# Seven-product gate and up blocks in three more feed-forward halves, and adaLN steps placed by an account of VectorE time

## The chip, the cores and the metric

One core of one Trainium2 chip runs the whole program. The metric is device time in microseconds (us) of one execution; medians are over repeated runs. TensorE (PE) does the matmuls, VectorE (DVE) and ScalarE (ACT) the elementwise work, GpSimd (POOL) a few small steps, and SyncE (SP) issues nearly all DMAs.

## The reference

Two layers over x of 512 tokens by 1024 channels, in float32. Each layer is a feed-forward half-step, a mixer (a convolution module in layer 0, pooling and block attention in layer 1), and a second feed-forward half-step. Every one of these sub-layers is normalised, shifted and scaled by vectors that come from a conditioning vector c (adaLN):

```
cond = silu(c)
for i in range(2):
    mod = (cond @ ada_w[i] + ada_b[i]).reshape(1, 3, 3, 1024)       # shift, scale, gate of 3 sub-layers
    h = rms_norm(x, ffn_norm[i, 0]) * (1 + mod[:, 0, 1]) + mod[:, 0, 0]
    x = x + 0.5 * mod[:, 0, 2] * ((silu(h @ w_gate) * (h @ w_up)) @ w_down)    # 1024 -> 2816 -> 1024
    ... mixer with mod[:, 1], then the second feed-forward half with mod[:, 2]
out = rms_norm(x, final_norm)
```

The four feed-forward halves are called parts 1 to 4 here: parts 1 and 2 belong to layer 0, parts 3 and 4 to layer 1. `ada_w` is 1024 x 9216 for each layer: nine chunks of 1024 columns, two of which (shift and scale of the first half) are computed at the start of the program.

## The kernel before, in words

Activations are kept transposed, as eight tiles of 128 channels by 512 tokens. Every operand of a matmul is split in a high and a low part (`hh`/`hl`, `th`/`tl`, `whi`/`wlo`), and each product is three matmuls: high by high, high by low, low by high (`mac`, L269). ScalarE makes the high part of a weight tile (L258), VectorE the low part (L260).

A feed-forward half is done in three sections of 8, 6 and 8 strips of 128 of the 2816 columns (`SECTIONS`). In a section each gate and each up strip is an item of 24 matmuls over 512 tokens (8 tiles x 3), then eight down items follow, 24 matmuls each (18 in the section of six strips). The post of an up item multiplies by silu of gate and splits the result into `th` and `tl` (L650 to L652); the post of a down item adds to x (L928), and in the last section also starts a sum of squares (L512). The last two down items belong to the boundary, which computes the next norm.

`run` (L131) writes out the order by hand: it walks a plan of steps, and every engine executes its own instructions in the order in which they were emitted. Before an item's matmuls it runs deferred work (`tick`), and issues the splits of up to three items ahead (`AHEAD`), with four weight tiles (`W_BUFS`). Loads of 1 MB go to four raw buffers (`RAW_BUFS`) on SP's queue, in the order in which they are first used; load i waits until load i-4 has been used.

An adaLN chunk is seven steps (`ada_steps`, L438): four that each multiply two rows of weights by c and add them up on VectorE (L454, L456), a fold (transpose L467, reduce L469), an empty one, and one that sums over partitions with a matmul (L474), which is followed by small adds (`put_mod`, L482). These steps are put between items as background: `body` (L935) hands out one after each item until the list is empty.

Part 4 already computes gate and up of 16 of its 22 strips as seven-product blocks (`pair_run`, L764): gate and up by the two halves of the 1024 channels, times those halves by two halves of the tokens, is a 2 x 2 by 2 x 2 product, made with seven products instead of eight. A product is 4 tiles x 3 matmuls over 256 tokens (`seventh`, L747), so a block is 84 matmuls of 256 columns where gate and up together are 48 of 512. VectorE makes the sums of weights and splits them (L727 to L744), subtracts and adds the products (L798, L805), and multiplies (L817). The sums of activations are made once per half, by `forms` (L691), and the first block of a run is prepared by `lead_in` (L829) beside the items ahead of it.

Of the kernel before, what the change touches and what calls it, by code (L numbers as in the profile page):

```python
# [14 lines left out]
P = 128  # L15
# [13 lines left out]
AHEAD = 3  # L29
# [38 lines left out]
class Trunk:  # L68
# [62 lines left out]
    def run(self):  # L131
# [6 lines left out]
        for dry in (True, False):  # L138
# [27 lines left out]
            ring = []  # L166
            for st in self.plan:
# [145 lines left out]
    def setup(self):  # L313
# [8 lines left out]
        cp = self.cp  # L322

# [23 lines left out]
        crow = cp.tile([8, P], F32, name="crow")  # L347
# [6 lines left out]
        par = cp.tile([P, P], F32, name="par")  # L354
        taps = cp.tile([A_CONV * 4, P], F32, name="taps")
        adab = cp.tile([72, 2, P], F32, name="adab")
# [81 lines left out]
    def ada_steps(self, l, s, ch):  # L438
# [97 lines left out]
    def apply(self, i, k, sl, rb):  # L536
# [3 lines left out]
        if n == S:  # L540
            t = self.fp.tile([P, n], F32, name=f"t{n}", tag="t512", bufs=3)
# [134 lines left out]
    def pair_items(self, l, s, first):  # L676
# [14 lines left out]
    def forms(self, kk):  # L691
# [8 lines left out]
        t = [self.fp.tile([P, 2, 256], F32, name="yy", tag="yy", bufs=2) for _ in range(2)]  # L700
# [4 lines left out]
        for e in range(2):  # L705
            hi = self.fp.tile([P, 2, 256], F32R, name=f"fh{kk}{e}", tag=f"fh{kk}{e}", bufs=1)
            lo = self.fp.tile([P, 2, 256], F32R, name=f"fl{kk}{e}", tag=f"fl{kk}{e}", bufs=1)
# [56 lines left out]
    def pair_run(self, pairs, prev, nxt, down, bg=()):  # L764

        nc = self.nc
        low = lambda p, n: (lambda: p.lows[n]())
        half = lambda p, n, c: (lambda: self.split_half(p, n, self.flat(p)[:, c * S:(c + 1) * S]))

        def begin(p):  # L770
            self.plan.append(("call", lambda: self.sums13(p), [p.raw]))

        def put_a(p):
            self.plan.append(("slot", p.a, lambda: self.split_full(p, ("a11", "a12"), self.flat(p)[:, 0:1024])))

        def put_c(p):
            self.plan.append(("slot", p.c, lambda: self.split_full(
                p, ("s3", "s1"), p.s13.rearrange("p a b -> p (a b)"))))
# [18 lines left out]
        def u2(p):  # L797
            nc.vector.tensor_tensor(p.x[:, 256:512], p.x[:, 256:512], p.p1, op=ALU.subtract)  # L798
            p.y = self.fp.tile([P, 2, 256], F32, name="yy", tag="yy", bufs=2)
# [25 lines left out]
        def do(*fns):  # L825
            for fn, *args in fns:
                self.call(lambda fn=fn, args=args: fn(*args))

        def lead_in(p):  # L829

            return [lambda: (begin(p), put_a(p), do((low(p, ("a11", "a12")),))),
                    lambda: (do((self.sum2, p), (half(p, "s2", 0),), (self.sum4, p)),),
# [864 lines left out]
```

## Time and profile before

| | us |
|---|---|
| median of 3 runs (1911.03 to 1911.79) | 1911.08 |
| the profiled execution | 1910.01 |
| its span, first to last instruction | 1908.2 |
| TensorE busy | 1856.6 |
| VectorE busy | 1183.8 |
| ScalarE busy | 681.3 |

The span is what the trace shows; the execution's own time is 1.8 us more. Busy times are unions of an engine's instructions. Matmuls are pipelined, so their durations overlap, and distances between their starts say more than durations. In a timeline the first number is the start, the second the duration; in brackets stands the idle time of the engine before it and what ended it.

### The profile page before, as it was taken

The page shows a single profiled execution, that of the slowest core. Times are in us where ns is not written, and L with a number is a line of the kernel's source. Part 1 is how long each engine was busy: PE and PEld are TensorE (multiplying, and loading weights), DVE is VectorE, ACT ScalarE, POOL GpSimd, SP SyncE. Part 2 cuts the span into 40 slices and gives each one's busy share as a digit, 9 for nine tenths or more (in the row PEclk, how much of TensorE's full clock was granted, in tenths as well). Part 3 has the DMA queues.
Part 4 walks back from the last instruction along what each step waited for, and adds up shares of the span by engine and source line. Part 5 has one row for each costly group of instructions (what it writes and reads, how often), then busy time and mean ns, then how long its engine had stood idle before and what let it go on. Part 6 is the DMA issues. An engine that isn't in the chain of part 4 may idle for free.

```text
span 1908.2 us, 22872 instructions
## 1 busy us (share of the span) xinstructions
PE 1856.6 (97%) x9290; PEld 1534.0 (80%) x9290; DVE 1183.8 (62%) x1652; ACT 681.3 (36%) x1084; POOL 131.8 (7%) x107
## 2 busy tenths in 40 slices
PE   5999999999979999999999999999999999999998
PEld 4788888888768888888888888888876688898997
DVE  6666676468976666663366643333757577576874
ACT  4321222235544322222242222223554444253553
POOL 2100000005550000000000000000102000000000
PEclk7999999999989999999999999999999999999999
DMA  9556656423221566562326542323122122424231
GB/s 252 171 203 214 205 195 215 158 67 111 67 88 45 199 216 200 201 199 89 111 67 221 200 142 78 110 89 107 54 84 71 45 89 67 133 62 138 79 100 45
DMA packets 221617, 247.29 MB, mean 130 GB/s; under 512 B 4572, under 2 KB 202056, under 8 KB 221512
## 3 DMA queue, kind: packets, MB, share of 16 engines
q1 hardware_dynamic: 221380, 245.78, 40.3%
q8 instruction: 73, 1.20, 0.3%
q14 instruction: 32, 0.26, 0.0%
q10 hardware_dynamic: 132, 0.05, 0.0%
HBM read 243.72 MB, written 2.10 MB: 129 GB/s over the span
## 4 chain that ended last, share of the span: by engine, by line
PE 88%; DVE 7%; ACT 2%; DMA 1%; issue 1%; POOL 1%; SPq 0%; ACTq 0%; DVEq 0%; POOLq 0%
PE bank L273 26%; PE bank L275 25%; PE bank L274 25%; PE bank L758 7%; DVE hl L549 1%; DVE bank L1051 1%; PE bank L1318 1%; DMA raw<-in_ada_w_dram 1%; DVE wlo L260 1%; DVE t L544 1%; PE bank L1271 1%; PE bank L1297 1%; ACT whi L258 1%; DVE yb L983 0%; PE bank L1184 0%
## 5 line engine op out<-in xcount | busy, mean ns | idle before, releaser
L273 PE MATMUL bank<-hh,whi 128*128 128x512 f32 (+1 forms) x1504 | 575.8, 383 | 5.6 <-ACT hh L547 3.2
L274 PE MATMUL bank<-hl,whi 128*128 128x512 f32 (+1 forms) x1504 | 569.5, 379 | 8.1 <-DVE hl L549 8.1
L275 PE MATMUL bank<-hh,wlo 128*128 128x512 f32 (+1 forms) x1504 | 568.4, 378 | 2.5 <-DVE wlo L260 2.5
L260 DVE TENSOR_TENSOR wlo<-raw,whi 128x1024 fp32r<-128x1024 f32 (+1 forms) x275 | 334.6, 1223 | 154.6 <-ACT whi L258 153.0
L258 ACT CAST whi<-raw 128x1024 fp32r<-128x1024 f32 (+1 forms) x285 | 289.0, 1020 | 208.6 <-PE bank L274 182.4
L273 PE MATMUL bank<-th,whi 128*128 128x512 f32 (+1 forms) x896 | 336.1, 375 | 5.1 <-ACT whi L258 4.5
L275 PE MATMUL bank<-th,wlo 128*128 128x512 f32 (+1 forms) x896 | 333.1, 372 | 5.4 <-POOL wlo L260 5.4
L273 PEld LDWEIGHTS bank<-hh,whi 128*128 128x128 f32 x1504 | 284.1, 189 | 66.8 <-ACT hh L547 3.3
L274 PEld LDWEIGHTS bank<-hl,whi 128*128 128x128 f32 x1504 | 283.8, 189 | 66.6 <-DVE hl L549 9.6
L274 PE MATMUL bank<-tl,whi 128*128 128x512 f32 (+1 forms) x896 | 332.9, 372 | 0.2 <-DVE tl L1324 0.2
L275 PEld LDWEIGHTS bank<-hh,wlo 128*128 128x128 f32 x1504 | 283.7, 189 | 61.2 <-DVE wlo L260 3.7
L273 PEld LDWEIGHTS bank<-th,whi 128*128 128x128 f32 x896 | 169.0, 189 | 38.9 <-ACT whi L258 5.6
L275 PEld LDWEIGHTS bank<-th,wlo 128*128 128x128 f32 x896 | 169.0, 189 | 38.5 <-POOL wlo L260 6.6
L928 DVE SCALAR_TENSOR_TENSOR x<-bank,modG,x 128x512 f32<-128x512 f32 (+1 forms) x124 | 86.2, 699 | 183.2 <-PE bank L275 182.6
L274 PEld LDWEIGHTS bank<-tl,whi 128*128 128x128 f32 x896 | 169.4, 189 | 31.9 <-DVE tl L1324 0.5
L650 DVE TENSOR_TENSOR m<-bank,sg 128x512 f32<-128x512 f32 (+1 forms) x75 | 50.2, 670 | 185.7 <-PE bank L275 178.0
L651 ACT CAST th<-m 128x512 fp32r<-128x512 f32 (+1 forms) x75 | 45.3, 604 | 307.0 <-DVE m L650 307.0
L456 DVE SCALAR_TENSOR_TENSOR adaacc<-raw,cond,adaacc 128x1024 f32<-128x1024 f32 x112 | 143.5, 1282 | 2.3
L644 ACT ACTIVATE sg<-bank 128x512 f32<-128x512 f32 (+1 forms) x78 | 44.0, 564 | 222.1 <-PE bank L275 222.1
L526 POOL TENSOR_TENSOR rs<-ms,mhalf 128x2 f32<-128x2 f32 x12 | 8.4, 699 | 1551.2 <-DVE ms L525 1551.2
L508 ACT ACTIVATE sq<-x 128x512 f32<-128x512 f32 (+1 forms) x54 | 29.0, 537 | 127.1 <-DVE x L928 125.4
L547 ACT ACTIVATE hh<-t,modB 128x256 fp32r<-128x256 f32 (+1 forms) x88 | 45.5, 528 | 63.1 <-DVE t L544 63.1
(249 smaller groups left out, 1985.6 us busy)
## 6 DMA issues: line engine op xcount, KB each, us to landing
raw<-in_ada_w_dram SPq DMA_DIRECT2D x64, 1024.0 KB, 5.0
raw<-in_ffn_w_gate_dram SPq DMA_DIRECT2D x35, 1024.0 KB, 5.4
raw<-in_ffn_w_up_dram SPq DMA_DIRECT2D x35, 1024.0 KB, 6.4
raw<-in_ffn_w_down_dram SPq DMA_DIRECT2D x32, 1024.0 KB, 5.3
raw<-in_ffn_w_down_dram SPq DMA_DIRECT2D x16, 768.0 KB, 4.4
raw<-in_conv_w_in_dram SPq DMA_DIRECT2D x10, 1024.0 KB, 5.1
raw<-in_ffn_w_gate_dram SPq DMA_DIRECT2D x18, 512.0 KB, 4.3
raw<-in_ffn_w_up_dram SPq DMA_DIRECT2D x18, 512.0 KB, 5.3
```

Source lines behind the costliest of these rows:

```text
L258: self.nc.scalar.copy(hi[:, 0:n, :], w)
L260: low = lambda eng=eng, lo=lo, hi=hi, w=w, n=n: eng.tensor_tensor(lo[:, 0:n, :], w, hi[:, 0:n, :].bitcast(F32), op=ALU.subtract)
L273: nc.tensor.matmul(ps, lhsT=it.hi[k], rhs=xh[:, sl], start=start, stop=False)
L274: nc.tensor.matmul(ps, lhsT=it.hi[k], rhs=xl[:, sl], start=False, stop=False)
L275: nc.tensor.matmul(ps, lhsT=it.lo[k], rhs=xh[:, sl], start=False, stop=stop)
L456: nc.vector.scalar_tensor_tensor(acc, r.tile[:, j, :], self.cond[:, k:k + 1], acc, op0=ALU.mult, op1=ALU.add)
L547: nc.scalar.activation(self.hh[k][:, sl], t, AF.Identity, bias=b, scale=1.0)
L644: nc.scalar.activation(self.sg[slot][:, sl], ps[:, sl], AF.Silu)
L650: nc.vector.tensor_tensor(m[:, sl], ps[:, sl], self.sg[slot][:, sl], op=ALU.mult)
L651: nc.scalar.copy(self.th[slot][:, sl], m[:, sl])
L758: mm = lambda w, x, start=False: nc.tensor.matmul(ps, lhsT=w, rhs=x, start=start, stop=False, skip_group_check=True)
L928: nc.vector.scalar_tensor_tensor(self.x[d][:, sl], ps[:, sl], self.modG[:, i, d:d + 1], self.x[d][:, sl], op0=ALU.mult, op1=ALU.add)
```

## The change

Parts 1, 2 and 3 now call `swiglu_pairs` too, with 12, 16 and 14 blocks: the last n strips of each section, given as counts such as (2, 6, 8). Part 4 keeps its 16. The function `swiglu` is gone.

adaLN steps carry a cost in us of VectorE. `slack` is called behind each ordinary item with the time that is taken to be free there (3.7 for a gate or up item, 3.6 or 2.2 for a down item, less the cost of a `forms` or `lead_in` step put there, and 3.0 once behind a run of blocks), and hands out steps as long as the account covers their cost, at most two with a load at a time, none behind a fold. Steps go through a queue (`drain`), which issues them when their load has been issued; it is stopped during a run of blocks (`hold`). What is left at the end of a part is called one after another. Part 1 computes six chunks instead of seven, the convolution stage one instead of none, part 2 four instead of six, part 3 five instead of three. The fold is done in two halves of 512 columns with its reductions at once, and several tiles share tags or are smaller (`SPARE`, `yy`, `qhi`), so that the tiles of blocks and adaLN fit side by side.

```diff
+FOLD = 1.9
+SPARE = [f"f{i}" for i in range(16)]
...
+            ring, queue, held = [], [], False
+
+            def drain(every=False):
+
+                while queue and not held and (every or queue[0][2] is None or queue[0][2].tile is not None):
+                    _, fn, r, cost = queue.pop(0)
+                    if r is not None:
+                        uses[id(r)] -= 1
+                    fn()
+                    if cost == FOLD:
+                        if every:
+                            self.tick()
+                        else:
+                            break
+                    pump()
...
+                        drain()
...
+                elif st[0] == "beside":
+                    if dry:
+                        if st[2] is not None:
+                            touch(st[2])
+                    else:
+                        queue.append(st)
+                        drain()
+                elif st[0] == "hold":
+                    held = st[1]
+                elif st[0] == "sync":
+                    if not dry:
+                        drain(True)
...
-            steps.append((accumulate(r, kk), r))
+            steps.append((accumulate(r, kk), r, 2.3))
 
         def fold():
 
-            tr = self.fp.tile([P, D], F32, name="adatr", tag="adatr", bufs=2)
-            nc.vector.transpose(tr, st["acc"])
             st["r"] = r = self.fp.tile([P, 32], F32, name="adar", tag="adar")
-            self.defer(lambda: nc.vector.tensor_reduce(
-                r, tr.rearrange("p (b j) -> p b j", j=32), axis=AX.X, op=ALU.add))
+            for e in range(2):
+                tr = self.fp.tile([P, S], F32, name="yy", tag="yy", bufs=2)
+                nc.vector.transpose(tr, st["acc"][:, e * S:(e + 1) * S])
+                nc.vector.tensor_reduce(r[:, 16 * e:16 * e + 16], tr.rearrange("p (b j) -> p b j", j=32),
+                                        axis=AX.X, op=ALU.add)
 
         def reduce():
             ps = self.bank()
             nc.tensor.matmul(ps[:, 0:32], lhsT=self.sel, rhs=st["r"], start=True, stop=True)
             self.defer(lambda: self.put_mod(l, s, ch, ps))
 
-        steps.append((fold, None))
-        steps.append((lambda: None, None))
-        steps.append((reduce, None))
+        steps.append((fold, None, FOLD))
+        steps.append((lambda: None, None, 0.0))
+        steps.append((reduce, None, 0.5))
...
-    def pair_items(self, l, s, first):
+    def pair_items(self, l, s, counts):
 
         a, e = self.a, 0 if s == 0 else 1
         wg = a["ffn_w_gate"][l, e].rearrange("(k p) f -> p k f", p=P)
         wu = a["ffn_w_up"][l, e].rearrange("(k p) f -> p k f", p=P)
         out, f0 = [], 0
-        for nf in SECTIONS:
-            out.append([])
-            for q in range(nf):
-                if f0 + q >= first:
-                    cs = slice((f0 + q) * P, (f0 + q + 1) * P)
-                    out[-1].append(Pair(Raw([P, 2048], (wg[:, :, cs], wu[:, :, cs]), 2), q))
+        for nf, n in zip(SECTIONS, counts):
+            cs = [slice((f0 + q) * P, (f0 + q + 1) * P) for q in range(nf)]
+            out.append([Pair(Raw([P, 2048], (wg[:, :, cs[q]], wu[:, :, cs[q]]), 2), q)
+                        for q in range(nf - n, nf)])
...
+    def lead_in(self, p):
+
+        return [lambda: (self.begin(p), self.put_a(p), self.do((self.low_of(p, ("a11", "a12")),))),
+                lambda: self.do((self.sum2, p), (self.half_of(p, "s2", 0),), (self.sum4, p)),
+                lambda: (self.put_c(p), self.do((self.low_of(p, "s2"),))),
+                lambda: self.do((self.low_of(p, ("s3", "s1")),))]
...
-            for _ in range(2):
-                if bg:
-                    self.call(*bg.pop(0))
...
+    def slack(self, bg, free):
+
+        self.credit += free
+        some = 0
+        while bg and some < 2 and self.credit >= bg[0][2] and (self.room > 0 or bg[0][1] is None):
+            fn, raw, cost = bg.pop(0)
+            self.credit -= cost
+            self.room -= raw is not None
+            some += raw is not None
+            self.plan.append(("beside", fn, raw, cost))
+            if cost == FOLD:
+                break
+
+    def beside(self, items, todo, bg, free):
+
+        gap = len(items) - len(todo)
+        for n, it in enumerate(items):
+            self.mm(it)
+            fn, cost = todo[n - gap] if n >= gap else (None, 0)
+            if todo and n == len(items) - 4:
+                self.room = 2
+            if fn is not None:
+                fn()
+            self.slack(bg, free - cost)
+        self.room = len(bg)
+
+    def swiglu_pairs(self, secs, pairs, bg, skip, fn=None, due=0):
+
+
+        self.form, self.credit, self.room = {}, 0.0, len(bg)
+        end = len(bg) - due
+        forms = [(lambda kk=kk: self.call(lambda: self.forms(kk)), 6.5) for kk in range(4)]
+        lead = [list(zip(self.lead_in(ps[0]), (2.5, 1.4, 1.9, 1.2))) if ps else [] for ps in pairs]
         for n, ((gu, down), ps) in enumerate(zip(secs, pairs)):
+            nf, last = SECTIONS[n], n == len(secs) - 1
+            gu = gu[skip if n == 0 else 0:2 * (nf - len(ps))]
+            todo = lead[n] if gu else []
+            if n == 0 and ps:
+                todo = forms + [(None, 0)] * (len(gu) - 8) + todo
+            self.beside(gu, todo, bg, 3.7)
             if n == 0:
-                gu = gu[:4 * 3]
-                todo = [lambda kk=kk: self.call(lambda: self.forms(kk)) for kk in range(4)]
-                todo[4:4] = [lambda: None] * (len(gu) - skip - 8)
-                todo += self.pair_run(ps, None, None, None)
-                for it in gu[skip:]:
-                    self.mm(it)
-                    if todo:
-                        todo.pop(0)()
-                for fn in todo:
-                    fn()
-            self.pair_run(ps, True, None, down, bg)
-            items = down[2:] if n < len(secs) - 1 else down[2:6]
-            todo = self.pair_run(pairs[n + 1], None, None, None) if n < len(secs) - 1 else []
-            for m, it in enumerate(items):
-                self.mm(it)
-                if bg:
-                    self.call(*bg.pop(0))
-                if todo and m >= len(items) - 4:
-                    todo.pop(0)()
-
-    def pair_start(self):
-        self.form = {}
+                assert len(bg) <= end
+                self.plan.append(("sync",))
+            if ps:
+                self.plan.append(("hold", True))
+                self.pair_run(ps, down)
+                self.plan.append(("hold", False))
+                self.slack(bg, 3.0)
+            if fn is not None and last:
+                self.call(lambda: self.table(fn))
+            todo = []
+            if not last and len(pairs[n + 1]) == SECTIONS[n + 1]:
+                todo = lead[n + 1]
+            if n == 0 and not ps:
+                todo = forms + todo
+            self.beside(down[2 if ps else 0:6 if last else 8], todo, bg, 3.6 if nf == 8 else 2.2)
+        self.plan.append(("sync",))
+        while bg:
+            self.call(*bg.pop(0)[:2])
+            self.call(self.flush)
...
-        bg = self.ada_steps(0, 0, 2) + ada(0, 1) + ada(0, 2)
+        steps = lambda l, *sc: sum((self.ada_steps(l, s, ch) for s, ch in sc), [])
+        bg = steps(0, (0, 2), (1, 1), (1, 0), (1, 2), (2, 1), (2, 0))
+        bg.insert(6, (self.rest, None, 0.6))
+        self.swiglu_pairs(f[0, 0], self.pair_items(0, 0, (0, 4, 8)), bg, 7, AF.Sigmoid, 8)
...
+        bg = steps(0, (2, 2))
         for k in (6, 7, 0, 1, 2, 3):
             self.call(lambda: self.conv_tick(0, 0))
+            self.call(*bg.pop(0)[:2])
             if k == 3:
                 for _ in range(4):
                     self.call(lambda: (self.conv_tick(0, 0), self.flush()))
             self.outer(lead, k, None, False, k == 3)
         self.mm(zo[4])
+        self.call(*bg.pop(0)[:2])
         self.mm(zo[5])
...
-        bg = ada(1, 0) + ada(1, 1)
-        self.swiglu(g0, bg, 3)
+        bg = steps(1, (0, 1), (0, 0), (0, 2), (1, 1))
+        self.swiglu_pairs(g0, self.pair_items(0, 2, (2, 6, 8)), bg, 3)
         self.boundary(g0[-1][1][6:], 3, f[1, 0][0][0][:4], False)
-        bg = ada(1, 2)
-        self.swiglu(f[1, 0], bg, 3, AF.Exp)
+        bg = steps(1, (1, 0), (1, 2), (2, 1), (2, 0), (2, 2))
+        self.swiglu_pairs(f[1, 0], self.pair_items(1, 0, (2, 4, 8)), bg, 3, AF.Exp)
...
-        self.swiglu_pairs(f[1, 2], self.pair_items(1, 2, 6), [], 3)
+        self.swiglu_pairs(f[1, 2], self.pair_items(1, 2, (2, 6, 8)), [], 3)
...
```

## Rows read from the trace of the kernel before

**Rows 1.** The page, part 1: busy us, share of the span, instructions.

```profile
PE 1856.6 (97%) x9290; PEld 1534.0 (80%) x9290; DVE 1183.8 (62%) x1652; ACT 681.3 (36%) x1084; POOL 131.8 (7%) x107
```

**Rows 2.** Waits of TensorE: who waited for whom, us in total, times, longest.

```profile
PE bank L274 <- DVE hl L549: 8.1, 6, 1.6
```

**Rows 3.** Stretches: length, busy us by engine, granted clock, DMA share, GB/s.

```profile
620.00:690.00 70.00, 70.00 (x311) 56.82 (x310) 47.82 (x52) 21.57 (x30) 0.00 (x0) 1.00 0.66 218
...
1803.00:1823.00 20.00, 20.00 (x173) 20.00 (x172) 18.18 (x26) 11.93 (x24) 0.00 (x0) 1.00 0.42 116
...
561.00:575.00 14.00, 14.00 (x70) 11.53 (x69) 3.62 (x6) 4.86 (x8) 2.15 (x2) 1.00 0.26 83
...
549.00:553.00 4.00, 3.70 (x9) 2.94 (x10) 3.59 (x5) 0.24 (x1) 2.57 (x2) 0.50 0.61 191
...
90.00:130.00 40.00, 40.00 (x176) 32.14 (x175) 26.47 (x31) 11.31 (x15) 0.00 (x0) 1.00 0.65 223
```

**Rows 4.** Timeline of TensorE, start and duration, ordinary items of part 4.

```profile
1564.04 0.40 PE L274 MATMUL bank<-hl,whi 128*128 128x512 f32 x1
...
1581.54 0.39 PE L274 MATMUL bank<-hl,whi 128*128 128x512 f32 x1
```

**Rows 5.** Timeline of TensorE, first matmuls of two successive blocks.

```profile
1801.54 0.28 PE L758 MATMUL bank<-hh,whi 128*128 128x256 f32 x1
...
1811.36 0.28 PE L758 MATMUL bank<-hh,whi 128*128 128x256 f32 x1
```

**Rows 6.** Timeline of TensorE, starts of the first two runs of blocks.

```profile
1619.67 0.28 PE L758 MATMUL bank<-hh,wlo 128*128 128x256 f32 x1
1620.85 0.39 PE L758 MATMUL bank<-fh,whi 128*128 128x256 f32 x1 [0.90 <-ACT yy L801]
...
1685.30 0.28 PE L758 MATMUL bank<-hh,wlo 128*128 128x256 f32 x1
1685.86 0.39 PE L758 MATMUL bank<-fh,whi 128*128 128x256 f32 x1 [0.29 <-ACT yy L801]
```

**Rows 7.** Timeline of VectorE, down items of part 2 with adaLN steps.

```profile
707.12 0.74 DVE L454 TENSOR_SCALAR adaacc<-raw,cond 128x1024 f32<-128x1024 f32 x1
...
709.10 1.22 DVE L260 TENSOR_TENSOR wlo<-raw,whi 128x1024 fp32r<-128x1024 f32 x1
...
712.05 0.75 DVE L928 SCALAR_TENSOR_TENSOR x<-bank,modG,x 128x512 f32<-128x512 f32 x1 [1.73 <-PE bank L275]
712.72 2.60 DVE L456 SCALAR_TENSOR_TENSOR adaacc<-raw,cond,adaacc 128x1024 f32<-128x1024 f32 x2
715.24 1.22 DVE L260 TENSOR_TENSOR wlo<-raw,whi 128x1024 fp32r<-128x1024 f32 x1
```

**Rows 8.** Timeline of VectorE, part 2: a fold, and the small adds.

```profile
701.30 0.68 DVE L491 SCALAR_TENSOR_TENSOR modA<-bank,adabT 32x8 f32<-32x8 f32 x4
...
702.09 1.22 DVE L260 TENSOR_TENSOR wlo<-raw,whi 128x1024 fp32r<-128x1024 f32 x1
...
729.52 1.24 DVE L467 STREAM_TRANSPOSE adatr<-adaacc 128x1024 f32<-128x1024 f32 x1
...
731.93 1.22 DVE L260 TENSOR_TENSOR wlo<-raw,whi 128x1024 fp32r<-128x1024 f32 x1
```

**Rows 9.** Timeline of VectorE behind the last blocks of part 4.

```profile
1862.74 1.46 DVE L928 SCALAR_TENSOR_TENSOR x<-bank,modG,x 128x512 f32<-128x512 f32 x2 [6.62 <-PE bank L275]
1864.89 0.69 DVE L512 TENSOR_TENSOR acc<-acc,sq 128x512 f32<-128x512 f32 x1 [0.70 <-ACT sq L508]
1865.83 2.36 DVE L260 TENSOR_TENSOR wlo<-raw,whi 128x1024 fp32r<-128x1024 f32 x2 [0.24 <-ACT whi L258]
```

**Rows 10.** Timeline of TensorE behind two long waits, conv stage.

```profile
549.89 0.63 PE L273 MATMUL bank<-th,whi 128*128 128x512 f32 x1
550.32 0.63 PE L274 MATMUL bank<-tl,whi 128*128 128x512 f32 x1
```

**Rows 11.** The page, part 2: GB/s in 40 equal slices of the span.

```profile
GB/s 252 171 203 214 205 195 215 158 67 111 67 88 45 199 216 200 201 199 89 111 67 221 200 142 78 110 89 107 54 84 71 45 89 67 133 62 138 79 100 45
```

More of the change, by code (lines that the diff above doesn't have):

```diff
@@ L322, in setup @@
         cp = self.cp
+        self.open_phase()
+        rows = lambda n, c, name, i: self.fp.tile([P, S], F32, name=name, tag=SPARE[9 + i], bufs=1)[0:n, 0:c]
         self.ident = cp.tile([P, P], F32, name="ident")
@@ L344, in setup @@
         self.tl = [cp.tile([P, S], F32R, name=f"tl{k}") for k in range(8)]
-        crow = cp.tile([8, P], F32, name="crow")
+        crow = rows(8, P, "crow", 0)
         nc.sync.dma_start(crow, a["c"].rearrange("o (k p) -> (o k) p", p=P))
@@ L353, in setup @@
                     nc.sync.dma_start(self.xin(c, h), xv[:, c, h * S:(h + 1) * S])
-        par = cp.tile([P, P], F32, name="par")
-        taps = cp.tile([A_CONV * 4, P], F32, name="taps")
-        adab = cp.tile([72, 2, P], F32, name="adab")
+        par = rows(P, P, "par", 1)
+        taps = rows(A_CONV * 4, P, "taps", 2)
+        adab = rows(72, 2 * P, "adab", 3).rearrange("p (a b) -> p a b", a=2)
         views = [
@@ L699, in forms @@
         b21, b22 = h[:, 1, 0:256], h[:, 1, 256:512]
-        t = [self.fp.tile([P, 2, 256], F32, name="yy", tag="yy", bufs=2) for _ in range(2)]
+        t = [self.fp.tile([P, S], F32, name="yy", tag="yy", bufs=2).rearrange("p (a b) -> p a b", a=2) for _ in range(2)]
         nc.vector.tensor_tensor(t[0][:, 0, :], b12, b11, op=ALU.subtract)
@@ L762, in seventh, with begin, put_a, put_c @@
             mm(p.lo[name][:, kk, :], xh)
[L764 to L778, printed above, removed]
+    def begin(self, p):
+        self.call(lambda: self.sums13(p), p.raw)
+    def put_a(self, p):
+        self.plan.append(("slot", p.a, lambda: self.split_full(p, ("a11", "a12"), self.flat(p)[:, 0:1024])))
+    def put_c(self, p):
+        self.plan.append(("slot", p.c, lambda: self.split_full(
+            p, ("s3", "s1"), p.s13.rearrange("p a b -> p (a b)"))))
+    def low_of(self, p, n):
+        return lambda: p.lows[n]()
+    def half_of(self, p, n, c):
+        return lambda: self.split_half(p, n, self.flat(p)[:, c * S:(c + 1) * S])
+    def do(self, *fns):
+        for fn, *args in fns:
+            self.call(lambda fn=fn, args=args: fn(*args))
+    def lead_in(self, p):
[3 more added lines that the diff above has]
+                lambda: self.do((self.low_of(p, ("s3", "s1")),))]
+    def pair_run(self, pairs, down):
+        nc, do = self.nc, self.do
+        begin, put_a, put_c, low, half = self.begin, self.put_a, self.put_c, self.low_of, self.half_of
         def product(p, name, bank, part, first=False, slot=None):
@@ L823, in put_tl @@
             nc.vector.tensor_tensor(self.tl[p.slot], p.m, self.th[p.slot].bitcast(F32), op=ALU.subtract)
[L825 to L832, printed above, removed]
-                    lambda: (put_c(p), do((low(p, "s2"),))),
-                    lambda: do((low(p, ("s3", "s1")),))]
-        if prev is None:
-            return lead_in(pairs[0])
         for n, p in enumerate(pairs):
@@ L1429, in go @@
             def go():
-                st[d] = acc = [self.fp.tile([P, 2, P], F32, name=f"acc{e}", tag=f"acc{e}", bufs=3)
-                               for e in range(3)]
+                st[d] = acc = [self.fp.tile([P, S], F32, name=f"acc{e}", tag=SPARE[d % 3 * 3 + e], bufs=1)
+                               [:, 0:256].rearrange("p (a b) -> p a b", a=2) for e in range(3)]
                 for k in range(3):
@@ L1466, in build @@
         self.sg, self.rb = {}, {}
-        ada = lambda l, s: sum((self.ada_steps(l, s, ch) for ch in range(3)), [])
         f = {(l, s): self.ffn_items(l, s) for l in range(2) for s in (0, 2)}
@@ L1609, in table @@
         self.nc.scalar.activation(t, self.mhalf[:, 0:1], fn)
-    def swiglu(self, secs, bg, skip, fn=None):
-        for n, (gu, down) in enumerate(secs):
-            self.body(gu[skip:] if n == 0 else gu, bg)
-            if fn is not None and n == len(secs) - 1:
-                self.call(lambda: self.table(fn))
-            self.body(down if n < len(secs) - 1 else down[:6], bg)
-        while bg:
-            self.call(*bg.pop(0))
-            self.call(self.flush)
     def boundary_tail(self, secs, i, head):
```

17 lines of the change are left out of this document (5 added, 12 removed).

## The prediction

> **What bounds the kernel now.** I read the shares of busy time first: TensorE is busy 97% of the span, VectorE 62% [rows 1]. Then the waits of TensorE: the longest in total is 8.1 us [rows 2], so almost nothing is left to win by removing waits; only fewer or cheaper matmuls can shorten the span. Then stretches, since 62% is a mean: in an ordinary gate/up stretch with adaLN steps VectorE is busy 47.82 of 70 us, but among seven-product blocks of part 4 it is busy 18.18 of 20 us [rows 3]. The reader is to see that the blocks which save TensorE work nearly fill VectorE, and that the same engine does the adaLN steps.
>
> I call the four feed-forward halves parts 1 to 4 and write an adaLN chunk's seven steps as a0 to a3 (two weight rows each), F (fold), n (empty), R (a matmul on TensorE, then small adds on VectorE).
>
> **What the blocks save.** Ordinary 512-column matmuls start 17.50 us apart over 75 of them, 0.2333 us each [rows 4]. Gate and up of one 128-column strip are 48 of them: 11.20 us. A block is 84 matmuls of 256 columns; the first matmuls of two successive blocks stand 9.82 us apart [rows 5]. A block saves 1.38 us. The change adds 12, 16 and 14 blocks in parts 1 to 3: 42 x 1.38 = 58.0 us. Each run of blocks starts with a wait for the copies yy: 1.18 us between two starts in the first run of part 4, 0.56 in its later ones, against 0.12 [rows 6], so 1.06 and 0.45 lost. Parts 2 and 3 have one of the first kind and two of the second (1.96 each), part 1 two of the second (0.9): 4.8 us. Net 53.2 us.
>
> The Trainium skill (TensorE: Matmul & The Clock Gate, Back-to-back issue gap) gives 262 cycles for 256 columns and 518 for 512 at full clock, an estimate of 109 and 216 ns. By that a block would save 1.19 us and all 50 us; the rows say 58, and I take the rows.
>
> **What VectorE pays.** Prices as distances between starts: residual 0.67, a pair of adaLN rows 2.52, a0 1.98 [rows 7]; fold 2.41, the small adds after R 0.79 [rows 8] (the new fold does the same elements in halves; as four instructions between 2.3 and 2.7, I take 2.41). In a last section each residual also brings a sum of squares, 0.69, and two low parts follow the first residuals, 2.36 together where one alone takes 1.22: 1.14 each [rows 7, 9]. So a chunk costs 1.98 + 3 x 2.52 + 2.41 + 0.79 = 12.7 us, where the account books 11.6. A down item of 5.6 us leaves 5.6 - 0.67 - 1.14 = 3.8 us, as booked (3.6), but in a last section only 3.1. Being late is harmless for low parts, which are issued three items ahead (16.8 us). It is not for R: TensorE's matmuls start in the order in which they were issued, R stands one item behind F, and everything behind R waits. A second such point is the start of a run of blocks.
>
> I follow the account through the item lists (its credits fix which step stands behind which item) and count VectorE's work from the end T of the first two down items.
> - Part 2, last section: T + residuals 1.3, a1 a2 5.0, two sums 1.4, two lows 2.3, residual 0.7, a3 2.5 = 13.2; sum, low, residual, F: 18.1. R stands at 16.8 (three items): 1.4 us of wait. a0 a1, sum, small adds, low, residual, a2 a3: 33.5. Nothing is handed out after that, so F is called at once (35.9) and R right behind it. TensorE has finished its last item at 23.9: it stands still 12.0 us.
> - Part 1, last section, the same way: F ends at 13.1 against 11.2, 2.0 us; the last F ends at 33.4 against 24.5, 8.9 us.
> - Part 3, last section: no wait inside; the last F ends at 30.8 against 22.5, 8.4 us (rounding in).
> - Parts 2 and 3, second section (items of 4.2 us): two steps of 2.52 directly behind the blocks, then F one item later, so F ends 11.2 after T against 8.4: 2.9 us each.
> - Part 2 before its second run and part 3 before its third: an adaLN pair is handed out behind the last item, ahead of the subtraction that the first block needs for yy, which is not on time even now by the 0.45 us above [rows 6]: 2.5 us each.
> - Part 1, end of the first gate/up: VectorE is 6.6 us late by these sums and the next section needs the last tl after 5.1: about 2 us (m and tl at the 0.69 of a sum over as many elements).
> Sum: part 1 12.9, part 2 18.8, part 3 13.8: 45.5 us given back. Below it, nothing if VectorE were never late; above it, the steps that are put off because their load isn't issued, all to the end of the part.
>
> **The clock.** After two waits of some 4 us, the granted clock was 0.5 (1.2 GHz) in 549 to 553 us [rows 3] and eight matmuls started 0.43 us apart instead of 0.23 [rows 10]: 1.6 us. The three long waits at the ends of parts 1 to 3 get that each, 4.8 us. The waits of 2 to 3 us get nothing; with 1.6 for each of seven it would be 11 us more.
>
> **The other edits.** The chunk moved to the conv stage is 12.7 us of VectorE among instructions that leave it idle 10.4 of 14 us there [rows 3]: nothing, at most 4 us if the norm chain is stretched. Its four 1 MB loads, like all loads, go down SP's queue in the order of use, each when the buffer four loads earlier is free; ahead of gate/up strips in 512-byte pieces, which in part 4 took 0.42 of the DMA share at 116 GB/s [rows 3], that is spare. The smaller tiles and shared tags are written and read by the same in-order engines: nothing, because no reader of the old contents is later than the conv stage's end.
>
> **Sum.** 1910.01 (the profiled execution, span 1908.2) - 53.2 + 45.5 + 4.8 = 1907.1; the median of the runs lies 1.07 above that execution, so 1908.2.
>
> **Rivals.**
> A: VectorE keeps up. Then only what is strictly serial behind the last item counts: residual + a3 + F = 5.6 in part 1, residual + a2 a3 + F = 8.1 in part 2, residual + F = 3.1 in part 3: 16.8, and 3.2 for the clock after the two longer ones: 1911.1 - 53.2 + 20.0 = 1878. For it: with one pair per item VectorE idles between its instructions now, so small bursts are absorbed. Against: the account books 11.6 for 12.7. Even the serial part gone would give 1911.1 - 53.2 = 1858.
> B, slower: loads come late in part 1's first section. Twelve adaLN loads and 4.5 weight loads of 1.05 MB in nine items, 50.4 us, are 343 GB/s. Now 223 GB/s there take 0.65 of the DMA share [rows 3], which makes 343 at a full share: no reserve. It decides from the point where less is delivered. At 252 GB/s, the highest of the page's 40 slices [rows 11], the 17.3 MB take 68.7 us: 18 us more, 1926. Against: each load has three others ahead of its use, and weight tiles are split three items ahead. The Trainium skill (DMA: Bandwidth & Descriptors, Specifications) puts the HBM limit of a core at about 358 GB/s; by that 343 just fits and B costs nothing. No stretch of this trace reaches either.
>
> **How the numbers follow.** Forecast (savings mostly given back as waits behind late VectorE work) 0.57, its own range 1893 to 1922; A 0.25; B 0.15; the full 1858 0.03. About 0.2% (3.8 us) is what a measurement can tell from no change. The forecast's 0.57 splits 0.22 faster, 0.18 same, 0.17 slower; A and 1858 are faster, B slower: 0.50, 0.18, 0.32. The range runs from 1872 (A with 6 us to spare) to 1926 (B).
>
> **What would show it.** Right: block periods of 9.8 us in parts 1 to 3; TensorE waiting 8 to 12 us for adar just ahead of each of the three boundaries, with the granted clock at 0.5 behind it; 2 to 3 us for adar in the second sections of parts 2 and 3; TensorE's idle time up by some 45 us. Wrong: no wait on adar over 5 us (A), or VectorE idle with a load of ada_w as releaser in part 1 (B); block periods above 10 us would make the first step wrong.

## The result: slower, 1924.24 us

| | before | after |
|---|---|---|
| median, us (lowest to highest, 4 runs each) | 1911.43 (1911.03 to 1912.77) | 1924.24 (1922.64 to 1927.18) |
| profiled execution, its span | 1910.01, 1908.2 | 1923.61, 1921.8 |
| part 1 / convolution / part 2 / part 3, us | 347.1 / 184.2 / 375.0 / 374.3 | 349.0 / 185.5 / 377.7 / 382.8 |

The ratio is 1.0068, 95% interval 1.005 to 1.0085: slower by 0.7%, which is clear of the noise, where slightly faster was forecast. A stage in the last line runs from the end of one boundary's wait for hl to the end of the next; part 1 begins at the matmul that sums squares, at 72.0 us before and 71.1 after.

The first lines of the page of after (busy time, share, instructions; then the granted clock in 40 slices):

```profile
span 1921.8 us, 26826 instructions
PE 1817.9 (95%) x10802; PEld 1580.7 (82%) x10802; DVE 1450.3 (75%) x2116; ACT 808.9 (42%) x1402; POOL 133.0 (7%) x107
...
PEclk7999999989989999999989999999999999999999
```

TensorE is busy 38.7 us less than before and VectorE 266.5 us more [rows 1], yet the span is 13.6 us longer: TensorE's idle time is up by 38.7 and 13.6, 52.3 us (forecast: some 45). What it stood still for, the view of its waits says (total us, times, longest):

```profile
PE bank L506 <- DVE adar L501: 40.4, 10, 12.2
PE bank L788 <- ACT yy L847: 11.2, 11, 2.8
PE bank L303 <- DVE hl L581: 8.0, 6, 1.6
...
PE bank L303 <- DVE tl L684: 2.5, 1, 2.5
```

Before, hl led this list with 8.1 us [rows 2], and there was no line for adar. adar is the fold's result; L506 is the reduce matmul R. Here is the longest of these waits, at the end of part 2, first on VectorE and then on TensorE:

```profile
958.09 0.75 DVE L991 SCALAR_TENSOR_TENSOR x<-bank,modG,x 128x512 f32<-128x512 f32 x1
958.76 5.24 DVE L487 SCALAR_TENSOR_TENSOR adaacc<-raw,cond,adaacc 128x1024 f32<-128x1024 f32 x4
964.03 0.71 DVE L500 STREAM_TRANSPOSE yy<-adaacc 128x512 f32<-128x512 f32 x1
...
966.11 0.69 DVE L501 TENSOR_REDUCE adar<-yy 128x16 f32<-128x512 f32 x1
```

```profile
966.95 0.60 PE L506 MATMUL bank<-adar,sel 128*128 128x32 f32 x2 [12.24 <-DVE adar L501]
...
967.72 0.41 PE L303 MATMUL bank<-tl,whi 128*128 128x256 f32 x1
967.93 0.41 PE L304 MATMUL bank<-th,wlo 128*128 128x256 f32 x1
```

VectorE has no gap in these lines, four accumulating instructions and the fold stand behind the last residual, and TensorE's queue is stopped by a matmul of 32 columns. Behind it 256-column matmuls start 0.21 us apart, where blocks' matmuls of the same width start 0.117 apart [rows 5]. The stretches of that place (length, TensorE busy, granted clock, DMA share, GB/s) show that the clock falls while TensorE waits and is still low behind the wait:

```profile
954.00:967.00 13.00, 0.76 (x5) 0.68 0.84 286
967.00:973.00 6.00, 6.00 (x31) 0.55 0.35 112
973.00:984.00 11.00, 9.42 (x82) 1.00 0.01 1
```

The other waits for adar and yy of 2.6 us and more (the bracket is the idle time and what ended it):

```profile
403.74 0.61 PE L506 MATMUL bank<-adar,sel 128*128 128x32 f32 x2 [8.97 <-DVE adar L501]
...
749.16 0.51 PE L788 MATMUL bank<-f,whi 128*128 128x256 f32 x2 [2.77 <-ACT yy L847]
...
823.80 0.41 PE L506 MATMUL bank<-adar,sel 128*128 128x32 f32 x2 [2.68 <-DVE adar L501]
...
1126.76 0.63 PE L506 MATMUL bank<-adar,sel 128*128 128x32 f32 x2 [3.21 <-DVE adar L501]
...
1206.75 0.41 PE L506 MATMUL bank<-adar,sel 128*128 128x32 f32 x2 [2.68 <-DVE adar L501]
...
1233.98 0.50 PE L788 MATMUL bank<-f,whi 128*128 128x256 f32 x2 [2.81 <-ACT yy L847]
...
1350.24 0.60 PE L506 MATMUL bank<-adar,sel 128*128 128x32 f32 x2 [7.66 <-DVE adar L501]
```

### The profile page after: what moved, and what is told of

It reads as the page before. It is cut to its first block, busy times and chain, and to the rows that moved or that the text cites. A ratio compares the mean times of both kernels' runs of the same rounds, so it can differ in the third digit from the quotient of the medians.

```text
span 1921.8 us, 26826 instructions
## 1 busy us (share of the span) xinstructions
PE 1817.9 (95%) x10802; PEld 1580.7 (82%) x10802; DVE 1450.3 (75%) x2116; ACT 808.9 (42%) x1402; POOL 133.0 (7%) x107
## 4 chain that ended last, share of the span: by engine, by line
PE 75%; DVE 17%; ACT 3%; issue 2%; DMA 2%; POOL 1%; SPq 0%; ACTq 0%; DVEq 0%; POOLq 0%
PE bank L788 27%; PE bank L302 15%; PE bank L304 14%; PE bank L303 14%; DVE adaacc L487 3%; DVE wlo L289 2%; DVE hl L581 1%; DVE x L991 1%; DVE bank L1114 1%; DMA raw<-in_ada_w_dram 1%; PE bank L1381 1%; DVE wlo L757 1%; DVE yy L500 1%; DVE adar L501 1%; DVE t L576 1%
## 5 line engine op out<-in xcount | busy, mean ns | idle before, releaser
L302 PE MATMUL bank<-hh,whi 128*128 128x512 f32 (+1 forms) x832 | 310.8, 374 | 5.3 <-ACT hh L579 3.2
L303 PE MATMUL bank<-hl,whi 128*128 128x512 f32 (+1 forms) x832 | 304.9, 366 | 8.0 <-DVE hl L581 8.0
L304 PE MATMUL bank<-hh,wlo 128*128 128x512 f32 (+1 forms) x832 | 304.0, 365 | 2.5 <-DVE wlo L289 2.5
L302 PEld LDWEIGHTS bank<-hh,whi 128*128 128x128 f32 x832 | 158.5, 191 | 36.6 <-ACT hh L579 3.3
L304 PEld LDWEIGHTS bank<-hh,wlo 128*128 128x128 f32 x832 | 158.0, 190 | 30.9 <-DVE wlo L289 3.7
L788 PE MATMUL bank<-f,whi 128*128 128x256 f32 x928 | 169.7, 281 | 11.2 <-ACT yy L847 11.2
L788 PE MATMUL bank<-f,qhi 128*128 128x256 f32 x928 | 173.2, 285 | 0.0
L788 PEld LDWEIGHTS bank<-f,whi 128*128 128x128 f32 x928 | 141.7, 188 | 13.4 <-ACT yy L847 13.4
L788 PEld LDWEIGHTS bank<-f,qhi 128*128 128x128 f32 x928 | 145.6, 193 | 0.0
L788 PE MATMUL bank<-f,qlo 128*128 128x256 f32 x464 | 132.0, 284 | 0.0
```

The source lines that it names most:

```text
L302: nc.tensor.matmul(ps, lhsT=it.hi[k], rhs=xh[:, sl], start=start, stop=False)
L303: nc.tensor.matmul(ps, lhsT=it.hi[k], rhs=xl[:, sl], start=False, stop=False)
L304: nc.tensor.matmul(ps, lhsT=it.lo[k], rhs=xh[:, sl], start=False, stop=stop)
L788: mm = lambda w, x, start=False: nc.tensor.matmul(ps, lhsT=w, rhs=x, start=start, stop=False, skip_group_check=True)
```

## The experiments

Each is compared with the kernel before on the same chip, whose medians there were 1910.96 to 1911.76.

### The blocks without the adaLN chunks

```diff
-        bg = steps(0, (0, 2), (1, 1), (1, 0), (1, 2), (2, 1), (2, 0))
-        bg.insert(6, (self.rest, None, 0.6))
+        bg = [(self.rest, None, 0.6)]
...
-        bg = steps(1, (0, 1), (0, 0), (0, 2), (1, 1))
+        bg = []
```

> The changed kernel without the adaLN chunks that run beside parts 1 to 3 and the convolution: their loads, VectorE steps and reduce matmuls are left out and the modulation vectors hold a constant, so the output is not the model's. The blocks stay. Theory (the blocks save what was worked out, 53 us, and all that was given back is TensorE waiting behind late VectorE work and running at half clock behind those waits): 1858 us, between 1850 and 1866, and no reduce wait and no half-clock stretch in parts 1 to 3. Rival (the blocks' own added sums and lows make VectorE the bound, or the blocks' products run slower than the ones of part 4): 1880 us or more, with waits for tl, yy or the lows left in the parts.

Measured 1859.22 us (1858.04 to 1862.4), ratio 0.9735 (0.972 to 0.975): 51.9 us below before. The wait for yy:

```profile
PE bank L790 <- ACT yy L849: 6.2, 11, 0.9
```

The theory holds in the main: no wait for adar is left, the wait for yy is down from 11.2, and the blocks give about what was worked out. By stages of the profiled executions, parts 1 to 3 are 12.9, 21.1 and 17.4 us shorter than before (worked out: 15.7, 20.1 and 17.4). Of that, 3.7 us are the 16 reduces that are left out, 0.23 us each on TensorE's queue before; against it stands one stretch at half clock in part 1, which was not expected, at 92 us, behind a wait of 2.08 us for the parameter rows, whose step comes earlier without the chunks. The convolution stage took 4.5 us more in this execution, with a second stretch at half clock. The 65.0 us between this and the changed kernel are what the adaLN steps cost there.

### What a wait costs beyond its length

```diff
+            elif getattr(self, "probe", None) and n % 3 == 2:
+                self.call(lambda p=self.probe.pop(0): self.wait_of(*p))
...
+    def wait_of(self, full, part):
...
+        t = self.fp.tile([P, D], F32, name="adaacc", tag="adaacc", bufs=1)
+        nc.vector.memset(t, 0.0)
+        for _ in range(part):
+            nc.vector.tensor_scalar(t, t, self.cond[:, 0:1], None, op0=ALU.mult)
+        for _ in range(full):
+            nc.vector.scalar_tensor_tensor(t, t, self.cond[:, 1:2], t, op0=ALU.mult, op1=ALU.add)
+        ps = self.bank()
+        nc.tensor.matmul(ps[:, 0:32], lhsT=self.sel, rhs=t[:, 0:32], start=True, stop=True)
...
```

> The kernel before, with 13 made-up waits in part 3, behind every third item: VectorE does a memset and a chain of 1.26-us and 0.75-us steps on a tile, then TensorE does one small matmul on it. The chains are 0.75, 1.3, 2.0, 2.5, 3.8, 5.0, 7.6 us long and then once more up to 5 us, so the waits are about that long. It measures what a wait of a given length costs beyond itself. Theory from the changed kernel's trace (stretches of 3.4 to 6.8 us at half clock behind waits of 3 us and more): behind the shortest two no half clock; behind those of 2.5 us and more 3 to 7 us at half clock, which is 1.7 to 3.0 us of lost time a wait, nearly the same for a wait of 2.5 us as for one of 7.6. Rival (the charge in the prediction: 1.6 us, and only behind waits of 8 us and more): full clock behind all waits up to 5 us.

One run: 1990.15 us. Stretches of TensorE from the made-up matmul on (columns as above):

```profile
1132.00:1140.00 8.00, 8.00 (x36) 1.00 0.32 100
...
1172.70:1182.00 9.30, 9.30 (x42) 1.00 0.03 8
...
1238.40:1248.00 9.60, 9.60 (x31) 0.69 0.00 0
...
1296.00:1303.00 7.00, 7.00 (x19) 0.55 0.01 2
1316.70:1326.00 9.30, 9.30 (x42) 1.00 0.18 63
...
1359.50:1364.00 4.50, 4.50 (x14) 0.62 0.17 58
```

The waits did not come out as long as their chains (the first chain of 1.3 us gave 3.66, the second 0.93), so they go by what was measured. Ahead of these six, in this order, TensorE started nothing for 0.31, 1.72, 7.69, 3.04, 0.93 and 2.25 us (the idle time in a bracket is some 0.4 less). Behind the three below 1.8 the clock stayed at 1.00, 2.4 GHz; behind the other three, and behind the other seven of 3.66 to 7.60 us, it was at 0.5, 1.2 GHz, for a while. Counted by the distance of starts (0.43 for 512 columns instead of 0.2333 [rows 4, 10]), and without the first matmul behind a wait, the slow matmuls cost 1.0 to 2.5 us a wait, 18.5 us behind the ten, and not more behind long waits: 1.55 behind 2.25 us, 2.5 behind 3.04, 2.3 behind 7.69. The theory holds and the rival falls: among these waits, one of 2 to 3 us nearly doubles its price.

### The account without the blocks

```diff
-        self.swiglu_pairs(f[0, 0], self.pair_items(0, 0, (0, 4, 8)), bg, 7, AF.Sigmoid, 8)
+        self.swiglu_pairs(f[0, 0], self.pair_items(0, 0, (0, 0, 0)), bg, 7, AF.Sigmoid, 8)
```

(and so in parts 2 and 3)

> The changed kernel with no seven-product blocks in parts 1 to 3 (all their items by the ordinary products, as before), so that the running account with its two-step limit and its new order of reduce and fold is alone. Theory (the account itself is cheap while VectorE has the time of 42 more full items): 1913 us, between 1909 and 1918, with one or two reduce waits left at ends of parts. Rival (the account as such, by putting a reduce in front of late VectorE work, loses the time whatever the blocks do): 1922 us or more, with reduce waits of 8 us and more at the ends of parts 1 to 3 as in the changed kernel.

Measured 1934.89 us (1933.75 to 1938.17), ratio 1.0131 (1.0116 to 1.0146). My expectation fell, and the rival's time came, though not with its mark: the ends of the parts are clean, the waits stand inside. Waits of TensorE, and the longest of them with the stretches from it on:

```profile
PE bank L506 <- DVE adar L501: 10.0, 6, 6.3
...
PE bank L303 <- DVE tl L684: 6.2, 3, 2.1
```

```profile
192.61 0.60 PE L506 MATMUL bank<-adar,sel 128*128 128x32 f32 x2 [6.26 <-DVE adar L501]
```

```profile
186.20:192.60 6.40, 0.15 (x1) 0.72 0.75 259
192.60:198.00 5.40, 5.39 (x18) 0.70 0.64 221
```

Both kernels run the same 7368 ordinary matmuls, so the n-th start can be compared with the n-th: of the 24.6 us by which the last of them starts later, 14.2 are there at 200 us, 6.8 of them at this one wait. VectorE is busy 1191.9 us of 1932.7 and still late: the account bunches steps. That is not a lack of VectorE time.

### The reduce one item later

```diff
         def reduce():
+            self.defer(go, 2)
+
+        def go():
             ps = self.bank()
```

> The changed kernel with one edit: the reduce matmul of an adaLN chunk is put one more item later on TensorE's queue (3.7 us more for VectorE to finish the fold). Theory (inside the parts the reduce is one item too early; at the ends the fold itself is late by 8 to 13 us and all deferred work is flushed there): the interior waits of 1.4, 1.5, 0.7, 3.1, 0.8, 3.6 and 3.1 us go, and with them four half-clock stretches, about 14 + 7 us; the end waits of 9.4, 12.6 and 8.1 us stay. 1905 us, between 1900 and 1912. Rival (VectorE is behind throughout, so whoever waits next takes the same time): 1920 us or more, the waits come back as tl, yy or longer end waits.

Measured 1906.49 us (1905.41 to 1910.75, 10 runs), ratio 0.9982 (0.9972 to 0.9991), as expected, and 17.8 us below the changed kernel. Ten waits for adar became three, the ones at the ends (the wait for yy at the start of part 2's second run did not go: 3.73 us here, 2.77 in the changed kernel):

```profile
PE bank L509 <- DVE adar L501: 28.3, 3, 12.0
```

### The end of part 2 handed on to part 3

```diff
+        if carry:
+            return
         self.plan.append(("sync",))
...
-        bg = steps(1, (1, 0), (1, 2), (2, 1), (2, 0), (2, 2))
+        bg += steps(1, (1, 0), (1, 2), (2, 1), (2, 0), (2, 2))
```

> The kernel with the late reduce (1906.5 us) with one edit more: the steps still unplaced at the end of part 2 (they wait 12.3 us there, all flushed) are not flushed but go on in part 3's account, ahead of its own chunks. Theory (an end wait costs its length and the half clock behind it): the 12.3 us and a 13.7-us stretch at half clock go, 18 us; part 3 has some 5 us of VectorE work more and its end wait grows from 7.2 to about 10 us: 1892 us, between 1886 and 1898. Rival (VectorE's work is what counts, wherever it is): part 3's end wait takes all of it, 1903 us or more.

Measured 1906.28 us (1901.72 to 1909.47, 9 runs), ratio 0.9972 (0.9961 to 0.9984): nothing gained over the kernel with the late reduce, the rival's time. (In the two profiled executions part 2 is 7.9 us shorter and part 3 3.9 us longer, as the edit would have it, but part 1, which it does not touch, is 3.2 us longer; so a gain of some us in parts 2 and 3 is not excluded.) The long wait for adar is gone from part 2, but two sums of 5.24 us still stand there ahead of the boundary's residual, and the next boundary matmul waits for x:

```profile
PE bank L509 <- DVE adar L501: 18.9, 2, 9.5
...
PE bank L302 <- DVE x L996: 5.7, 1, 5.7
```

### The account put right: prices and free times alone, then places too

```diff
-FOLD = 1.9
+FOLD = 2.6
...
-            steps.append((accumulate(r, kk), r, 2.3))
+            steps.append((accumulate(r, kk), r, 2.5 if kk else 2.0))
...
-            self.beside(down[2 if ps else 0:6 if last else 8], todo, bg, 3.6 if nf == 8 else 2.2)
+            self.beside(down[2 if ps else 0:6 if last else 8], todo, bg, 2.6 if nf == 6 else 2.9 if last else 3.7)
```

> The changed kernel with only the prices and free times of the account put right from the trace (first sum 2.0, other sums 2.5, fold 2.6, reduce 0.8, forms 4.2, third lead edit 0.7; free 2.6 an item of the six-deep section, 2.9 of the last); order of steps, places and limits as they were. Tells whether the wrong prices or the places (reduce one item behind its fold, nothing at the runs' ends) made the waits. Theory (places): interior reduce waits of 1 to 3.6 us mostly stay, the end waits shrink to 3 to 6 us since the last section's items are handed no more than they hold: 1905 us, between 1892 and 1918. Rival (prices): 1880 us or less.

Prices and free times alone: 1892.74 us (1892.32 to 1894.17), ratio 0.9903 (0.9886 to 0.9919), 31.5 us below the changed kernel. That is between the two forecast times, at the lower edge of the theory's range: wrong prices and free times made two thirds of the 46.7 us that the second kernel has back. Which of them did it, those booked too low or those booked too high (forms, 6.5 for 4.2), was not taken apart. Its waits for adar are 12.7 us in 8 (40.4 in 10 before the edit).

The second kernel has places too (a chunk's reduce goes behind the next chunk's third sum):

```diff
+                if late is not None:
+                    sums.insert(3, late)
...
         do((silu2, p), (mult, p), (put_th, p), (put_tl, p))
+        self.plan.append(("hold", False))
+        self.credit = min(self.credit, 0.0)
+        self.slack(bg, free)
```

> The changed kernel with the account put right from the trace: prices a first sum 2.0, other sums 2.5, fold 2.6, reduce 0.8, forms 4.2, third lead edit 0.7; free time 2.6 an item of the six-deep section and 2.9 of the last one; the account set back to nothing at each run's end, and the steps for that place handed out ahead of the two down products that end the run, where VectorE stood idle for 3.8 to 6.6 us, instead of behind them; the queue emptied ahead of every run; each chunk's reduce placed behind the next chunk's third sum. All blocks and all 21 background chunks stay. By its account one reduce is left at each part's end instead of three to eight steps. Theory (TensorE's waits behind late steps and the half clock behind them are all that was given back): 1866 us, between 1858 and 1878; waits for adar under 6 us in all, no half-clock stretch inside the parts beside the ones that the kernel before has. Rival (VectorE, 1450 us busy, has no room for the chunks beside 88 blocks wherever they are put): 1890 us or more, the waits come back as tl, yy or lows.

1877.57 us (1874.68 to 1882.35), ratio 0.9824 (0.9808 to 0.9841), at the upper edge of what was expected (there are 16 chunks beside the parts, not the 21 of that text). Busy times, and the longest wait; adar has none:

```profile
PE 1804.0 (96%) x10802; PEld 1571.6 (84%) x10802; DVE 1451.5 (77%) x2116; ACT 808.9 (43%) x1402; POOL 133.3 (7%) x107
...
PE bank L788 <- ACT yy L847: 16.9, 11, 3.0
```

VectorE does the same work as in the changed kernel (1451.5 against 1450.3 us) in a span 48.9 us shorter. That refutes the rival. What is left sits at four run starts, with a stretch at half clock behind three of them, which the expectation had not; VectorE and TensorE at one of them:

```profile
824.47 1.21 DVE L757 TENSOR_TENSOR wlo<-s,whi 128x1024 fp32r<-128x1024 f32 x1
825.60 0.70 DVE L500 STREAM_TRANSPOSE yy<-adaacc 128x512 f32<-128x512 f32 x1
...
831.15 0.42 DVE L844 TENSOR_TENSOR bank<-bank,p1c 128x256 f32<-128x256 f32 x1
```

```profile
832.30 0.50 PE L788 MATMUL bank<-f,whi 128*128 128x256 f32 x2 [2.96 <-ACT yy L847]
```

A fold (four instructions from 825.60 on) stands ahead of the first block's subtraction, on which yy waits.

### Run starts cleared, then the last reduce handed on

```diff
-            self.slack(bg, free - cost)
+            if not todo or n < len(items) - 1:
+                self.slack(bg, free - cost)
```

> The kernel with the account put right (1877.6 us) with one edit: no adaLN step behind the last item ahead of a run (there a fold of 2.8 us stood in front of the first block's sums, and TensorE waited 3.24 us for yy with a 3.4-us half-clock stretch behind, four times); the fold goes to the run's end, and the end of the last run is handed 7.0 us in place of 5.0. Theory (such a wait is the fold's delay, and costs 2.1 us over the 1.18 of the undisturbed runs and 1.7 of clock): three to four of them go, 11 to 15 us; part 2 ends with a reduce directly behind its fold, which waits about 3 us plus 1.7 of clock: 1868 us, between 1862 and 1873. Rival (the waits come back at the runs' ends, where the two steps now sit in front of the first residual): 1875 us or more.

1877.75 us (1875.52 to 1880.89), ratio 0.9827 (0.9813 to 0.984): nothing gained, the rival's time. The yy waits went as expected (16.9 to 6.2 us; half clock had stood behind three of the four, not behind all), and as much came back, not at the residuals but at the ends of the parts, where the steps that had moved were now late:

```profile
PE bank L506 <- DVE adar L501: 9.6, 3, 4.4
...
PE bank L788 <- ACT yy L847: 6.2, 11, 0.9
```

The last kernel issues those three reduces behind the first item of the next stage:

```diff
         for n, it in enumerate(z[3:]):
             self.mm(it)
+            if n == 0:
+                self.call(bg[-1][0])
```

> The kernel with the cleared run starts (1877.75 us) with one edit: the one reduce left at each end of parts 1 to 3 is not issued there, one item or none behind its fold, but behind the first item of the stage that follows (in part 3 by its account). No VectorE work is moved, only the matmul of 32 columns and its small adds. Theory (an end wait is the matmul's place on TensorE's queue and costs its length and the half clock behind it): the end waits of 3.06, 4.76 and 2.98 us go, 10.2 us without the steps of an undisturbed matmul, and with them half-clock stretches of 6.8, 3.4 and 3.4 us, 6.8 us: 1861 us, between 1856 and 1867. Rival (the boundaries behind the parts wait for VectorE anyway, as it still has the fold to do): 1872 us or more, with the waits back as hl, hh or x.

1874.46 us (1870.27 to 1878.31), ratio 0.9804 (0.9788 to 0.982): the lowest median of the kernels with all chunks, but 3.3 us instead of 17, and the two intervals of the ratio overlap. No wait for adar is left; the boundary's matmuls wait instead, for a residual that stands behind the same sums and fold:

```profile
PE bank L302 <- DVE x L990: 6.5, 3, 2.8
```

At a part's end VectorE itself is late (2.8, 1.0 and 2.8 us), and whichever matmul is next pays.

## Why the prediction was wrong

**The blocks: right.** First matmuls of two successive blocks in part 3 of after, 9.82 us apart as in part 4 before [rows 5]:

```profile
1258.10 0.28 PE L788 MATMUL bank<-hh,whi 128*128 128x256 f32 x1
...
1267.92 0.28 PE L788 MATMUL bank<-hh,whi 128*128 128x256 f32 x1
```

**The waits behind late VectorE work: right in place, kind and sum, but for one.** Forecast and measured idle, us:

| | forecast | measured |
|---|---|---|
| part 1: tl, reduce inside, end | 2.0, 2.0, 8.9 | 2.5, 1.1, 8.97 |
| part 2: run start, second section, last section, end | 2.5, 2.9, 1.4, 12.0 | 2.77, 2.68, 0.4, 12.24 |
| part 3: first section | none | 3.21 |
| part 3: second section, run start, end | 2.9, 2.5, 8.4 | 2.68, 2.81, 7.66 |
| sum | 45.5 | 47.1 |

The sum for part 2 (33.5) holds a sum, a low part and a residual, 2.5 us, that its list leaves out; the trace has them. The wait that was not forecast stands in part 3 at 1126.76. I had an item between the chunk's last two sums and its fold; on VectorE they follow each other behind one residual:

```profile
1117.99 0.75 DVE L991 SCALAR_TENSOR_TENSOR x<-bank,modG,x 128x512 f32<-128x512 f32 x1 [2.28 <-PE bank L304]
1118.66 5.24 DVE L487 SCALAR_TENSOR_TENSOR adaacc<-raw,cond,adaacc 128x1024 f32<-128x1024 f32 x4
1123.93 0.71 DVE L500 STREAM_TRANSPOSE yy<-adaacc 128x512 f32<-128x512 f32 x1
```

**The clock: the step that failed.** "The waits of 2 to 3 us get nothing": wrong. Stretches behind the reduces at 1126 and 1206 and the run start at 749:

```profile
1126.00:1133.00 7.00, 6.24 (x16) 0.51 0.86 276
...
1207.00:1211.50 4.50, 4.50 (x15) 0.62 0.80 192
750.50:754.00 3.50, 3.50 (x19) 0.51 0.49 137
```

Seven of the nine waits of 2.5 us and more in the table have such a stretch; those at 143 (tl) and 823.80 have none. By the distances of starts the slow matmuls cost 2.1, 1.5, 2.1, 2.3, 1.55, 1.55 and 1.65 us, in order of time: 12.9 in all, where 4.8 was charged. The three ends, charged with 1.6 each, took 5.9; the four shorter waits, charged with nothing, took 7.0. The prediction named the alternative, 11 us more, and gave no reason against it; the rows that it shows have half clock only behind waits of some 4 us [rows 3, 10]. The trace of before had a shorter one, at the start of the program:

```profile
44.94 0.50 PE L275 MATMUL bank<-hh,tl 128*128 128x512 f32 x1 [2.44 <-DVE tl L260]
...
46.57 0.63 PE L275 MATMUL bank<-hh,tl 128*128 128x512 f32 x1
46.99 0.63 PE L273 MATMUL bank<-hh,th 128*128 128x512 f32 x1
```

The last two starts are 0.42 us apart instead of 0.23. The made-up waits bear it out: of those from 2.25 us on, ten of ten. In the kernels themselves it is not always so: of 22 idle times of 2 to 3 us in parts 1 to 3 of all the kernels here but the one with made-up waits, 14 have half clock behind them and 8 have none; behind every longer one it is there. The Trainium skill (TensorE: Matmul & The Clock Gate, HAM oscillation — how this bites in real kernels) describes a kernel that pays the clock's way back once per wait for a DMA; the changed kernel's trace agrees, for seven of nine waits behind late VectorE work, with 1.5 to 2.3 us each.

**The sum.** 1924.24 less 1908.2 is 16.0 us. The clock is 8.1 of it, the unforeseen reduce 3.2. Some 3.5 more are small: a reduce at 107 us that waited 1.1, two runs of parts 1 and 3 that began like the first kind (1.18 between starts) where I took the second (0.6 each), and 1.2 in the convolution stage, costed at nothing with at most 4. The other waits came out 1.6 below their forecast; about 3 us I can't place. The direction of the forecast hung on little: 53.2 saved less 50.3 given back (45.5 and 4.8) left 2.9 us.

**The rivals.** A, VectorE keeps up, was wrong for this kernel, but its 1878 is what the corrected account reaches (1877.57): VectorE can do the work beside the blocks, handed out otherwise. That the numbers meet is chance: A has 16.8 us of waits at the parts' ends, the corrected kernel none for adar there and 10.7 us more for yy at run starts than the kernel without chunks. "An account that books 11.6 for 12.7" was the point to press; with the prices and free times put right, the kernel is faster than before. B is refuted: in the first section of part 1 the loads came at 315 GB/s, above the 252 on which B's price was built, and VectorE waits nowhere for a background chunk's row:

```profile
92.00:142.00 50.00, 47.98 (x209) 38.30 (x207) 47.56 (x60) 12.86 (x17) 0.00 (x0) 1.00 0.90 315
```

In this row VectorE, the third engine, is busy 47.56 of 50 us, and TensorE's two waits of 1 us and more in that section are for VectorE's work (adar at 107 us, tl at 143); no matmul there waits for a load.

**What stays open.** Of the 15.2 us between the best kernel and the one without chunks (1874.46 and 1859.22), the waits at the three ends are 6.5, the half clock behind two of them some 4 and the 16 reduces themselves 3.7; the wait at 92 us, which only the kernel without chunks has, stands against that with 3.6. The rest was not taken apart. Why the wait of 2.68 us at 823.80 left the clock alone and the one of 2.68 at 1206.75 didn't was not tried.

## What to carry to other kernels

When a bounded engine gets background work by a book of its time, take prices and free times from distances between starts in the trace: putting them right alone (by 0.2 to 0.7 us a step of a chunk, 1.2 for a lead-in step and 2.3 for the forms) was worth 31.5 us here. Keep an instruction that waits on such work (a matmul of 32 columns) at least two items behind it. Moving the work away from the points where a serial chain begins gained nothing by itself: it came back at the ends. Price a wait of TensorE above 3 us at its length and 1 to 2.5 us more, and one of 2 to 3 us so too, since in two of three cases here it cost that. To see whether an engine is out of time or only badly served, compare its busy time in two placements: 1450 us of VectorE went with 1924 us and with 1874.

## What the runs showed of the hardware that was not expected

Among the made-up waits the granted clock did not fall behind 0.31, 0.93 and 1.72 us without a start, and fell behind every one from 2.25 us on. In the kernels themselves it fell behind 14 of 22 idle times of 2 to 3 us in parts 1 to 3. In the convolution stage of four kernels it fell behind less: behind an idle time of 1.7 us that came some 2.5 us after another of about 1 us (in the kernel without chunks, 0.98 ending at 541.20 and 1.70 ending at 543.64; so too in the one with places and the last two). What it costs to come back did not grow with the wait (1.55 us behind 2.25, 1.67 behind 7.44). And loads ran at 315 GB/s over 50 us at 0.90 of the DMA share, well above the highest slice of before [rows 11].
